# A diffusion backbone on one core: where the modulation steps stand in VectorE's order, where one of their vectors is computed, and which queue loads their tiles

## Chip, cores and metric

The kernel runs on one core of a Trainium2 chip. The metric is device microseconds of one execution; the median of three runs of the kernel before is 2502.87 us (2501.15 to 2503.94). A profile is one further execution, taken by the hardware profiler; it has its own time.

Five engines matter: TensorE (PE, matmuls; PEld is its weight load), VectorE (DVE), ScalarE (ACT), GpSimd (POOL), which here does little but issue DMAs, and SyncE (SP), which issues nearly all other DMAs. Each runs its own instructions in the order in which they were laid down and waits on semaphores for the others.

## The reference, cut to what matters

Two layers over 512 latent and 256 context tokens of width 1024. Every sub-layer is an RMSNorm with a scale and a shift, a body, and a gated residual; shift, scale and gate come out of one product of a conditioning vector with a large matrix, `ada_w`:

```python
m_lat = (silu_c @ ada_w[i] + ada_b[i]).reshape(b, N_SUBLAYERS, N_MOD, 1, d)
m_ctx = (silu_cc @ ada_w[i] + ada_b[i]).reshape(N_SUBLAYERS, N_MOD, 1, d)
h = norm_modulate(x_lat, norm_g[i, 0], m_lat[:, 0, 0], m_lat[:, 0, 1])
x_lat = x_lat + MACARON_WEIGHT * m_lat[:, 0, 2] * swiglu(h, ffn_w_in[i, 0], ffn_w_out[i, 0])
```

Layer 0 is SwiGLU, short convolution, SwiGLU; layer 1 is SwiGLU, attention, SwiGLU. So there are 2 x 9 modulation vectors of 1024 numbers (shift, scale and gate of three sub-layers in two layers), each for two conditioning rows, latent and context, but for the last four of layer 1, which only the latent tokens need.

## The kernel before, in words

**Stages.** The program runs through six stages in this order: f00 (first SwiGLU), c01 (convolution), f02, f10 (SwiGLUs), attention, and the last SwiGLU. In the profile f00 ends near 585 us, c01 near 837, f02 near 1353, f10 near 1877 us; attention and the last SwiGLU follow.

**Products.** The four stages f00, c01, f02 and f10 go through `products` (from line 1014). A stage has column chunks of 128 outputs (22 in an FFN stage, 12 in the convolution). The first two or three chunks are done directly; each of the others is seven products, M1 to M7, in the manner of Strassen: 12 matmuls each over four 128-row blocks and three parts (high x high, high x low, low x high), 384 tokens wide. In a chunk's order M7, M4 and M3 come one chunk later than M1, M2, M5 and M6. In an FFN stage every product but M1, M5 and M6 is followed by an eviction on DVE: L1069 after M2, L1078 after M7, L1129 after M4, L1083 after M3. L1078 must be done before M4 goes on in the same PSUM bank; L1083 frees a bank of tag C.

**Second projections.** After two or four chunks (convolution: four of its own outputs) stands a step `out`: the second projection of what is ready, 8 output blocks in groups of 3, 3 and 2, each for the latent tokens (512 wide) and then the context tokens (256 wide). That makes six groups of matmuls with DVE evictions at L874. `out_steps` is a generator that yields after each of the six; `out_phase` runs it through.

**Weights.** SP loads raw weight tiles (L209, five buffers, 512 KB each). `split` (L179 on ACT, L180 on DVE) makes high and low parts, a granule; eight granules are held ahead of PE. L347 and L356 form the sums and differences that M3, M5 and M6 need. PE and SP keep the order of the program; DVE and ACT are ordered by a scheduler at build time, which lets an instruction go ahead as soon as it takes its inputs to be there.

**Modulation steps.** The 15 vectors that are not needed at the start are computed on DVE beside the products. A vector is 8 blocks of 128 outputs, each block in two halves of 512 inputs; a half block is one tile `aw` (128 x 512, 256 KB) and one or two steps, `ada_block` (line 497): L505 multiplies the tile with a conditioning row (`crow`) and adds up along the row, one step per conditioning row. A vector with two rows is 32 steps, with one row 16. `ADA_BY` (line 39) says how many of the 15 vectors are done by the end of a stage: 6 in f00, 4 more in f02, 5 more in f10; none in c01. `ADA_DEPTH` (line 40) is the number of tile buffers, 3 each. When the last step on a tile is traced, `ada_next` (line 490) issues the load that takes its buffer, on POOL's queue. Between the two halves stand 13 tasks that are no steps: the load of the other half of the rows, its Silu on ACT, and 11 that do nothing.

**Pace.** `bg` (line 554) is called once after every product and not in a second projection. From product 12 of the stage (its tiles are asked for two products sooner) to product `7 * (total - 2 - direct) - 1` it spreads the stage's tasks evenly: 205 tasks over 107 products in f00, 141 over 114 in f02, 109 over 114 in f10. Only the first step of a stage is pinned with `keep_in_program_order`, which puts an instruction behind the instruction that was traced on its engine just before; the others may be moved ahead or behind by the scheduler.

Of the kernel before, what the change touches and what calls it, by code (L numbers as in the profile page):

```python
# [9 lines left out]
F32 = mybir.dt.float32  # L10
# [7 lines left out]
P = 128  # L18
# [17 lines left out]

FFN_DIRECT, CONV_DIRECT, BOOT_DIRECT = 2, 3, 3

ADA_BY = {"f00": 6, "f02": 10, "f10": 15}
ADA_DEPTH = {"f00": 3, "f02": 3, "f10": 3}  # L40
HALF = D // 2
CONV_PARTS = (4, 4)
LAT, CTX = 0, 1
BOTH = ((0, NL), (NL, NX))
# [76 lines left out]
def backbone(ctx: ExitStack, tc: tile.TileContext, a: dict, out: bass.AP):  # L121
    nc = tc.nc
# [4 lines left out]
    tmp = ctx.enter_context(tc.tile_pool(name="tmp", bufs=4))  # L127
# [17 lines left out]
    def ptile(name, shape=(P, 512)):  # L145
        pool, tag = bank[name]
        return pool.tile(list(shape), F32, name=f"ps_{name}", tag=tag)
# [4 lines left out]
    vec, at = {}, 0  # L152
# [226 lines left out]
    def starts(parts):  # L379
        out = [0]  # L380
        for n in parts:
            out.append(out[-1] + n)
        return out
# [50 lines left out]
    ada_tasks, ada_range = {}, {}  # L434
# [53 lines left out]
    ada_blocks, ada_loaded, ahead = [], {}, {}  # L488

    def ada_next(n):  # L490

        if n < ahead["limit"]:
            i, m, k, c0 = ada_blocks[n]
            w = ada_loaded[n] = ahead["pool"].tile([P, HALF], F32, name=f"aw{i}_{m}_{k}_{c0}", tag="aw", bufs=ADA_DEPTH[ahead["key"]])
            nc.gpsimd.dma_start(w, a["ada_t"][i, m, k, :, c0 : c0 + HALF])  # L495

    def ada_block(n, v, nv):

        i, m, k, c0 = ada_blocks[n]
        w = ada_loaded[n]
        junk = w if v == nv - 1 else apool.tile([P, HALF], BF16, name=f"jk{n}", tag="acc")
        out = mods[i][:, m, k, v : v + 1]
        ins = dve.tensor_tensor_reduce(out=junk, in0=w, in1=ahead["rows"][:, v], scale=1.0, scalar=out if c0 else ada_b[:, i, m, k : k + 1], op0=ALU.mult, op1=ALU.add, accum_out=out)  # L505
        if pinned[0]:
            tc.keep_in_program_order(ins)
        pinned[0] = False
        if v == nv - 1:
            ada_loaded.pop(n)  # L510
            ada_next(n + ADA_DEPTH[ahead["key"]])
            if k == KC - 1 and c0:
                ada_done.update({(i, 2 * m), (i, 2 * m + 1)})

    def rows_load(c0):
        rows = ahead["rows"] = ahead["pool"].tile([P, 2, HALF], F32, name=f"crow{c0}", tag="crow")
        nc.gpsimd.dma_start(rows, a["c_rows"][:, c0 : c0 + HALF].partition_broadcast(P))

    def rows_silu():
        act.activation(ahead["rows"], ahead["rows"], AF.Silu)  # L520
# [1 line left out]
    def rest():  # L522
        pass

    pinned = [False]
    pace = {}

    def ada_list():

        vectors = [(i, m) for i in range(2) for m in range(9) if i or m > 2]  # L530
        t0 = 0
        for key, t1 in ADA_BY.items():
            first = len(ada_blocks)
# [9 lines left out]
            ada_range[key] = first, len(ada_blocks)  # L543
            t0 = t1

    def bg_start(key, pool, first, last):

        pace.update(n=0, done=0, first=first, last=last, tasks=ada_tasks.pop(key, []))
        pace["steps"] = len(pace["tasks"])
        if pace["steps"]:  # L550
            ahead.update(pool=pool, key=key, start=ada_range[key][0], limit=ada_range[key][1])
        pinned[0] = True

    def bg():

        pace["n"] += 1
        if not pace["steps"]:
            return
        if pace["n"] == pace["first"] - 6:
            rows_load(0)  # L560
        if pace["n"] == pace["first"] - 2:
            rows_silu()
            for n in range(ADA_DEPTH[ahead["key"]]):
                ada_next(ahead["start"] + n)
        if pace["n"] < pace["first"]:
            return
        span = pace["last"] - pace["first"] + 1
        due = min(pace["steps"], -(-pace["steps"] * (pace["n"] - pace["first"] + 1) // span))
        while pace["done"] < due:
            pace["tasks"][pace["done"]]()  # L570
            pace["done"] += 1
# [10 lines left out]
    stage = {}  # L582
# [413 lines left out]
    def out_phase(*args):  # L996
        for _ in out_steps(*args):
            pass
# [15 lines left out]
    def products(gp, key, order, parts, direct, chunk, straight, out_args, after, passes, hooks, hold):  # L1014


        live = {}
        at = starts(parts)
        total = at[-1]
        pairs = [0]  # L1020
        bg_start(key, stage["aw"], 10 if key == "c01" else 12, 7 * (total - 2 - direct) - 1)

        def directly(n, c, m):
            half, kh = int(m[0]), int(m[1])
            st = live.setdefault(c, {"taken": {}, "used": {}})
            if kh not in st["taken"]:
                mark = len(taken)
                st[kh] = [w_get(0) for _ in range(2)]
                st["taken"][kh] = taken[mark:]
                del taken[mark:]  # L1030
            if kh == 0:
                st["ps", half] = [ptile(t, (P, NH)) for t in ("BS" if pairs[0] == 3 else "AC")]
                pairs[0] += 1
            xh, xl = T[f"B{kh + 1}{half + 1}"]
            for k in range(4):
                for (wh, wl), ps in zip(st[kh], st["ps", half]):
                    mm3(ps, wh[:, k, :], wl[:, k, :], xh[:, k, :], xl[:, k, :], kh == 0 and k == 0, kh == 1 and k == 3)
                if (n, k) in hooks:
                    hooks[n, k]()
                if k == 2 and half:  # L1040
                    w_fill(1)
            st["used"][kh] = st["used"].get(kh, 0) + 1
            if st["used"][kh] == 2:
                taken.extend(st["taken"][kh])
                w_done()
            if kh == 1:
                evictions.append(lambda ps=st["ps", half]: straight(c, half, ps))
                if n not in hold:
                    evict()

        def product(c, m):
            st = live.setdefault(c, {})
            _, tname, tag = PRODUCTS[m]
            first = m in ("M1", "M2", "M5")
            if first:
                st[tag] = ptile(tag, (P, NH))
            ps = st[tag]
            wh, wl = w_get()
            th, tl = T[tname]
            for k in range(4):  # L1060
                mm3(ps, wh[:, k, :], wl[:, k, :], th[:, k, :], tl[:, k, :], first and k == 0, k == 3, skip_group_check=True)
            w_done()
            if c == total - 1:
                traced.add((key, m))
            if m == "M1":
                st["g1"] = qp.tile([P, NH], F32, name="g1", tag="g1", bufs=2)
                act.activation(st["g1"], ps, AF.Copy)
            elif m == "M2":
                dve.tensor_tensor(out=st["g1"], in0=ps, in1=st["g1"], op=ALU.add)  # L1069
            elif m == "M5":  # L1070
                st["c22"] = qp.tile([P, NH], F32, name="c22", tag="c22", bufs=2)
                act.activation(st["c22"], ps, AF.Copy)
            elif m == "M6":
                st["g2"] = qp.tile([P, NH], F32, name="g2", tag="g2", bufs=2)
                act.activation(st["g2"], ps, AF.Copy)
                chunk(c, "c11", st)
            elif m == "M7":
                dve.tensor_tensor(out=st["c22"], in0=ps, in1=st["c22"], op=ALU.add)  # L1078
                chunk(c, "c22", st)
            elif m == "M4":  # L1080
                chunk(c, "c21", st)
            else:
                dve.tensor_tensor(out=st["g2"], in0=ps, in1=st["g2"], op=ALU.add)  # L1083
                chunk(c, "c12", st)
                live.pop(c)

        steps = [n for n, (c, m) in enumerate(order) if m != "out" and c < direct]
        for n, (c, m) in enumerate(order):
            if m == "out":
                last = c == len(parts) - 1  # L1090
                if last and isinstance(after, dict):
                    out_close(*out_args(c), after)
                else:
                    out_phase(BOTH, passes, *out_args(c), after if last else None, out_banks, 3)
                    if n in hooks:
                        hooks[n]()
                    for go in behind_outs:
                        go()
                    behind_outs.clear()
            elif c < direct:  # L1100
                directly(n, c, m)
            else:
                product(c, m)
                bg()
            if n in hooks and m != "out":
                hooks[n]()
            if n == steps[-1]:
                free_order()
# [692 lines left out]
```

## Time and profile before

| what | value |
|---|---|
| median of three runs | 2502.87 us (2501.15 to 2503.94) |
| the profiled execution | 2499.04 us, span 2497.3 us, mean granted clock 0.994 |
| PE busy | 2436.3 us of the span, 13632 matmuls |
| L505, modulation steps | 416 steps, median 745 ns; 240 tiles, 256 KB each |
| steps run | 152 to 472 us (f00), 914 to 1139 (f02), 1430 to 1619 (f10) |
| DVE waits for a tile's DMA | 16.8 us in 19 waits |
| SP's raw loads in f00, 150 to 480 us | waited 308.4 us for splits |
| POOL's instructions | 254, nearly all of them DMA issues |

How to read it: busy times of engines overlap, so no sum of them is the span. `out<-in` names what an instruction writes and reads. A row of waits has the waiting engine and line, the one that released it, the total, the number and the longest wait. A row of windows has the stretch, its length, the busy time (and count) of PE, PEld, DVE, ACT and POOL, the clock that PE was granted (1.00 is full), the DMA engines' busy share and GB/s. A time line row has the start, the length, the engine, the line and the operation, and in brackets the idle time before it and what ended it. `DVEq`, `SPq` and the like are an engine's sequencer, which issues DMAs and waits.

### The profile page before, as it was taken

What the parts mean: (1) busy time and instruction counts of PE and PEld (TensorE: products, weight loads), DVE (VectorE), ACT (ScalarE), POOL (GpSimd) and SP (SyncE); (2) the same over time, 40 slices, a digit from 0 to 9 for tenths busy, and PEclk for the clock granted to TensorE, in tenths of its full rate; (3) what the DMA queues carried; (4) which work ended last, traced back from release to release, by engine and by line L of the source; (5) the groups of instructions that cost most, each with busy time, mean ns of one, the idle gap of its engine ahead of it and who ended that gap; (6) DMA issues with size and microseconds to landing.
All of it is one profiled execution on the core that took longest, in us unless ns stands there. A gap on an engine that the chain in (4) does not pass through costs nothing.

```text
span 2497.3 us, 35662 instructions
## 1 busy us (share of the span) xinstructions
PE 2436.3 (98%) x13632; PEld 2263.3 (91%) x13632; DVE 1897.2 (76%) x3758; ACT 1094.2 (44%) x2016; POOL 135.1 (5%) x254
## 2 busy tenths in 40 slices
PE   6999999999999999999999999999999999999998
PEld 3889999999999999999999999899997889888887
DVE  4699999878968899996667989866668887544443
ACT  4443343355525643433435534244346775433233
POOL 0011111000000001110000021200000000000000
PEclk9999999999999999999999999999999999999999
DMA  7333543330213034533221155522231101332221
GB/s 276 110 125 116 165 155 129 110 110 26 76 51 117 28 106 148 161 123 102 85 74 49 67 172 167 183 79 68 68 110 60 43 18 60 102 101 93 96 82 34
DMA packets 92155, 252.53 MB, mean 101 GB/s; under 512 B 10192, under 2 KB 19536, under 8 KB 91984
## 3 DMA queue, kind: packets, MB, share of 16 engines
q1 hardware_dynamic: 71072, 183.00, 22.3%
q0 software_dynamic: 20064, 66.08, 8.2%
q8 instruction: 107, 1.75, 0.3%
q10 hardware_dynamic: 848, 1.18, 0.1%
q14 instruction: 64, 0.52, 0.1%
HBM read 248.11 MB, written 2.10 MB: 100 GB/s over the span
## 4 chain that ended last, share of the span: by engine, by line
PE 74%; issue 11%; DVE 8%; ACT 2%; POOL 2%; DMA 2%; SPq 0%; POOLq 0%; DVEq 0%; ACTq 0%
PE ps_A L809 14%; PE ps_A L808 14%; PE ps_A L810 14%; PE ps_C L808 7%; PE ps_C L810 7%; PE ps_C L809 7%; POOL aw L495 2%; PE ps_B L810 2%; PE ps_B L809 2%; PE ps_B L808 2%; DVE w L180 2%; DVE aw L505 1%; DVE jk L505 1%; PE ps_T L1481 1%; DVE x L874 0%
## 5 line engine op out<-in xcount | busy, mean ns | idle before, releaser
L179 ACT ACTIVATE w<-raw 128x512 fp32r<-128x512 f32 (+2 forms) x810 | 491.5, 618 | 752.4 <-PE ps_A L810 460.3
L180 DVE TENSOR_TENSOR w<-raw,w 128x512 fp32r<-128x512 f32 (+2 forms) x810 | 541.2, 677 | 183.9 <-ACT w L179 175.2
L809 PE MATMUL ps_A<-gl,w 128*128 128x512 f32 (+2 forms) x624 | 212.6, 341 | 0.4 <-DVE gl L180 0.4
L808 PE MATMUL ps_A<-gh,w 128*128 128x512 f32 (+2 forms) x624 | 212.1, 340 | 0.1
L810 PE MATMUL ps_A<-gh,w 128*128 128x512 f32 (+2 forms) x624 | 212.0, 340 | 0.0
L495 POOL DMA_DIRECT2D aw<-in_ada_t x240 | 129.6, 540 | 1130.5 <-DVE mods L505 1109.6
L874 DVE SCALAR_TENSOR_TENSOR x<-ps_A,gat,x 128x512 f32<-128x512 f32 (+1 forms) x192 | 118.6, 619 | 79.7 <-PE ps_A L810 79.5
L808 PE MATMUL ps_C<-gh,w 128*128 128x512 f32 (+1 forms) x472 | 166.6, 353 | 9.1 <-DVE g L1083 8.8
L809 PE MATMUL ps_C<-gl,w 128*128 128x512 f32 (+1 forms) x472 | 165.9, 352 | 0.0
L810 PE MATMUL ps_C<-gh,w 128*128 128x512 f32 (+1 forms) x472 | 165.7, 351 | 0.0
L809 PE MATMUL ps_A<-hl,w 128*128 128x512 f32 (+1 forms) x424 | 162.6, 384 | 2.4 <-DVE hl L668 2.4
L808 PE MATMUL ps_A<-h,w 128*128 128x512 f32 (+1 forms) x424 | 162.2, 382 | 1.0 <-DVE x L874 1.0
L810 PE MATMUL ps_A<-h,w 128*128 128x512 f32 (+1 forms) x424 | 162.1, 382 | 0.0
L347 DVE TENSOR_TENSOR raw<-raw,raw 128x512 f32<-128x512 f32 x204 | 139.5, 687 | 8.8 <-DMA raw<-in_ffn_w_in 6.3
L809 PEld LDWEIGHTS ps_A<-gl,w 128*128 128x128 f32 x624 | 118.6, 190 | 16.0 <-DVE gl L180 1.9
L808 PEld LDWEIGHTS ps_A<-gh,w 128*128 128x128 f32 x624 | 118.5, 190 | 15.2 <-ACT gh L179 1.0
L810 PEld LDWEIGHTS ps_A<-gh,w 128*128 128x128 f32 x624 | 118.6, 190 | 12.9
L874 DVE SCALAR_TENSOR_TENSOR x<-ps_C,gat,x 128x512 f32<-128x512 f32 (+1 forms) x136 | 87.7, 645 | 52.0 <-PE ps_C L810 51.8
L808 PEld LDWEIGHTS ps_C<-gh,w 128*128 128x128 f32 x472 | 90.0, 191 | 22.5 <-issue 11.3
L808 PE MATMUL ps_A<-tB11h,w 128*128 128x384 f32 x312 | 106.9, 343 | 3.0 <-ACT tB11h L763 2.9
L809 PE MATMUL ps_A<-tB11l,w 128*128 128x384 f32 x312 | 106.1, 340 | 0.3 <-DVE tB11l L765 0.3
L810 PE MATMUL ps_A<-tB11h,w 128*128 128x384 f32 x312 | 105.7, 339 | 0.0
(426 smaller groups left out, 6623.9 us busy)
## 6 DMA issues: line engine op xcount, KB each, us to landing
raw<-in_ffn_w_in SPq DMA_DIRECT2D x174, 512.0 KB, 3.7
aw<-in_ada_t POOLq DMA_DIRECT2D x240, 256.0 KB, 3.2
raw<-in_ffn_w_out SPq DMA_DIRECT2D x76, 512.0 KB, 3.9
raw<-in_conv_w_in SPq DMA_DIRECT2D x24, 512.0 KB, 3.7
ada<-in_ada_w SPq DMA_DIRECT2D x27, 256.0 KB, 6.0
raw<-in_attn_w_qkv SPq DMA_DIRECT2D x12, 512.0 KB, 4.8
raw<-in_ada_w SPq DMA_DIRECT2D x8, 512.0 KB, 5.2
raw<-in_conv_w_out SPq DMA_DIRECT2D x8, 512.0 KB, 3.7
```

The costliest lines, as they stand in the source:

```text
L179: act.activation(dsth, src, AF.Copy)
L180: dve.tensor_tensor(out=dstl, in0=src, in1=dsth.bitcast(F32), op=ALU.subtract)
L347: dve.tensor_tensor(out=quad(o), in0=quad(x), in1=quad(y), op=ALU.subtract)
L495: nc.gpsimd.dma_start(w, a["ada_t"][i, m, k, :, c0 : c0 + HALF])
L505: ins = dve.tensor_tensor_reduce(out=junk, in0=w, in1=ahead["rows"][:, v], scale=1.0, scalar=out if c0 else ada_b[:, i, m, k : k + 1], op0 ...
L808: pe.matmul(ps, wh, xh, start=first, stop=False, **kw)
L809: pe.matmul(ps, wh, xl, start=False, stop=False, **kw)
L810: pe.matmul(ps, wl, xh, start=False, stop=last, **kw)
L874: dve.scalar_tensor_tensor(out=x, in0=p[:, o - off : o - off + w], scalar=gat[:, m, v : v + 1], in1=x, op0=ALU.mult, op1=ALU.add)
L1481: pe.transpose(pt[:, c, :], pr[:, (c0 + c) * P : (c0 + c + 1) * P], ident)
```

## The change

1. The vectors are divided otherwise: 5 in f00, 1 in c01, 4 in f02, 5 in f10. c01's tiles use two buffers of an existing pool (tag `r`).
2. Every step is pinned behind what was traced before it on DVE, not only the first of a stage.
3. `bg` is also called after each of the six groups of a second projection. A stage's tasks are spread over weights: 1 for each product, 6 and 3 in turn for the latent and the context group.
4. A tile's load is issued on SP's queue, not POOL's, and at the next call of `bg` (or when it is needed), not with the step that frees its buffer. The row loads (`crow`) stay on POOL's queue.

```diff
-ADA_BY = {"f00": 6, "f02": 10, "f10": 15}
-ADA_DEPTH = {"f00": 3, "f02": 3, "f10": 3}
+ADA_BY = {"f00": 5, "c01": 6, "f02": 10, "f10": 15}
+ADA_DEPTH = {"f00": 3, "c01": 2, "f02": 3, "f10": 3}
+OUT_WEIGHT = (6, 3)
...
-            w = ada_loaded[n] = ahead["pool"].tile([P, HALF], F32, name=f"aw{i}_{m}_{k}_{c0}", tag="aw", bufs=ADA_DEPTH[ahead["key"]])
-            nc.gpsimd.dma_start(w, a["ada_t"][i, m, k, :, c0 : c0 + HALF])
+            pool, tag = (tmp, "r") if ahead["key"] == "c01" else (ahead["pool"], "aw")
+            w = ada_loaded[n] = pool.tile([P, HALF], F32, name=f"aw{i}_{m}_{k}_{c0}", tag=tag, bufs=ADA_DEPTH[ahead["key"]])
+            nc.sync.dma_start(w, a["ada_t"][i, m, k, :, c0 : c0 + HALF])
...
+        while n not in ada_loaded:
+            ada_next(ada_freed.pop(0))
...
-        if pinned[0]:
-            tc.keep_in_program_order(ins)
-        pinned[0] = False
+        tc.keep_in_program_order(ins)
         if v == nv - 1:
             ada_loaded.pop(n)
-            ada_next(n + ADA_DEPTH[ahead["key"]])
+            ada_freed.append(n + ADA_DEPTH[ahead["key"]])
...
-    def bg():
-
-        pace["n"] += 1
+
+    def bg(at):
+
+        while ada_freed:
+            ada_next(ada_freed.pop(0))
         if not pace["steps"]:
             return
-        if pace["n"] == pace["first"] - 6:
+        first = min(pace["slots"])
+        if at == (first[0] - 6, 0):
             rows_load(0)
-        if pace["n"] == pace["first"] - 2:
+        if at == (first[0] - 2, 0):
             rows_silu()
             for n in range(ADA_DEPTH[ahead["key"]]):
                 ada_next(ahead["start"] + n)
-        if pace["n"] < pace["first"]:
-            return
-        span = pace["last"] - pace["first"] + 1
-        due = min(pace["steps"], -(-pace["steps"] * (pace["n"] - pace["first"] + 1) // span))
+        pace["now"] += pace["slots"].get(at, 0)
+        due = min(pace["steps"], -(-pace["steps"] * pace["now"] // pace["total"]))
         while pace["done"] < due:
             pace["tasks"][pace["done"]]()
             pace["done"] += 1
...
-        bg_start(key, stage["aw"], 10 if key == "c01" else 12, 7 * (total - 2 - direct) - 1)
+        begin, end = 10 if key == "c01" else 12, 7 * (total - 2 - direct) - 1
+        slots, count = {}, 0
+        for c, m in order:
+            if m == "out":
+                if begin <= count <= end:
+                    slots.update({(count, 1 + q): OUT_WEIGHT[q % 2] for q in range(6)})
+            elif c >= direct:
+                count += 1
+                if begin <= count <= end:
+                    slots[count, 0] = 1
+        bg_start(key, stage["aw"], slots)
+        traced_products = 0
...
-                    out_phase(BOTH, passes, *out_args(c), after if last else None, out_banks, 3)
+                    steps_of = out_steps(BOTH, passes, *out_args(c), after if last else None, out_banks, 3)
+                    for q, _ in enumerate(steps_of):
+                        bg((traced_products, 1 + q))
...
                 product(c, m)
-                bg()
+                traced_products += 1
+                bg((traced_products, 0))
```

More of the change, by code (lines that the diff above doesn't have):

```diff
@@ L523, in rest @@
         pass
-    pinned = [False]
+    ada_freed = []
     pace = {}
@@ L544, in ada_list, with bg_start @@
             t0 = t1
[L546 to L550, printed above, removed]
+    def bg_start(key, pool, slots):
+        tasks = ada_tasks.pop(key, [])
+        pace.update(tasks=tasks, steps=len(tasks), done=0, now=0, slots=slots, total=sum(slots.values()))
+        if tasks:
             ahead.update(pool=pool, key=key, start=ada_range[key][0], limit=ada_range[key][1])
-        pinned[0] = True
-    def bg():
-        pace["n"] += 1
+    def bg(at):
+        while ada_freed:
+            ada_next(ada_freed.pop(0))
         if not pace["steps"]:
             return
-        if pace["n"] == pace["first"] - 6:
+        first = min(pace["slots"])
+        if at == (first[0] - 6, 0):
             rows_load(0)
-        if pace["n"] == pace["first"] - 2:
+        if at == (first[0] - 2, 0):
             rows_silu()
```

## The prediction

> **What bounds the kernel now.** I read the page first (parts 1 and 2), then who TensorE (PE) waited for, stage by stage, then the time line of VectorE (DVE) just before PE's longest waits.
>
> ```profile
> PE 2436.3 (98%) x13632; PEld 2263.3 (91%) x13632; DVE 1897.2 (76%) x3758; ACT 1094.2 (44%) x2016; POOL 135.1 (5%) x254
> DVE  4699999878968899996667989866668887544443
> ```
>
> PE is busy for 98% of 2497.3 us, so an edit on DVE can win only PE's waits and the slow matmuls after them. The digits show DVE full in slices 3 to 7 (125 to 437 us, stage f00) and around slices 14 to 17 and 22 to 24 (f02, f10): the three stages that carry modulation steps. PE's waits on DVE in these stages (f00 150 to 480, f02 840 to 1120, f10 1400 to 1620 us; columns: total, times, longest):
>
> ```profile
> PE ps_A L808 <- DVE c L1078: 3.6, 1, 3.6
> PE ps_C L808 <- DVE g L1083: 2.6, 2, 2.2
> ...
> PE ps_C L808 <- DVE g L1083: 1.3, 1, 1.3
> ...
> PE ps_C L808 <- DVE g L1083: 4.9, 2, 3.8
> PE ps_A L808 <- DVE c L1078: 1.1, 1, 1.1
> ```
>
> That is 6.2 + 1.3 + 6.0 = 13.5 us. Both lines are evictions of a product, L1078 for M7 and L1083 for M3. PE waits again for the first when it begins M4, two products later; for the second when the second projection, which follows M3 at once, wants its second C bank. Why L1083 is late, from DVE's time line before the 3.8 us wait:
>
> ```profile
> 1561.02 0.74 DVE L505 CUSTOM_DVE_ANT_0 aw<-aw,crow,mods 128x512 f32<-128x512 f32 x1
> 1561.69 0.08 DVE L505 DVE_READ_ACCUMULATOR2_ANT mods<- 128x1 f32 x1
> 1561.69 0.55 DVE L1078 TENSOR_TENSOR c<-ps_A,c 128x384 f32<-128x384 f32 x1
> ...
> 1568.00 0.75 DVE L505 CUSTOM_DVE_ANT_0 aw<-aw,crow,mods 128x512 f32<-128x512 f32 x1 [1.48 <-DMA aw<-in_ada_t]
> 1568.68 0.08 DVE L505 DVE_READ_ACCUMULATOR2_ANT mods<- 128x1 f32 x1
> 1568.68 0.68 DVE L180 TENSOR_TENSOR w<-raw,w 128x512 fp32r<-128x512 f32 x1
> 1569.28 0.75 DVE L505 CUSTOM_DVE_ANT_0 aw<-aw,crow,mods 128x512 f32<-128x512 f32 x1
> ...
> 1572.17 0.55 DVE L1083 TENSOR_TENSOR g<-ps_C,g 128x384 f32<-128x384 f32 x1
> ```
>
> A step (L505) takes 0.67 us from its start to the next (1561.02 to 1561.69). Steps stand ahead of evictions that PE needs, and one of them sat 1.48 us waiting for its own tile with the queue behind it.
>
> A wait also slows the matmuls after it. Windows over the ends of three waits (columns: length, PE, PEld, DVE, ACT, POOL busy, granted clock, DMA share, GB/s):
>
> ```profile
> 178.40:181.40 3.00, 2.95 (x9) 2.95 (x10) 3.00 (x8) 0.00 (x0) 1.01 (x2) 0.50 0.51 167
> 188.00:191.50 3.50, 3.50 (x10) 2.68 (x11) 3.50 (x9) 0.81 (x2) 0.54 (x1) 0.55 0.24 77
> 1573.00:1578.00 5.00, 5.00 (x16) 3.92 (x17) 3.44 (x9) 0.80 (x2) 1.61 (x3) 0.66 0.87 298
> ```
>
> Lost work: 3.0 x 0.50 + 3.5 x 0.45 + 5.0 x 0.34 = 1.5 + 1.6 + 1.7 = 4.8 us. With the waits, 18.3 us are at stake. The middle window follows the 2.2 us wait. By the Trainium skill ("TensorE: Matmul & The Clock Gate", Part 1: The HAM clock gate) the clock halves only after an idle window of about 3.4 us; by that rule this 1.6 us would not belong to the wait and the stake would be 16.7 us. This trace does not agree, since its clock is 0.55 right behind a wait of 2.2 us, so I keep 18.3.
>
> **Pace and load, before and after.** Between its two halves a stage has 13 tasks that are no steps. Before, the tasks of a stage fell evenly on its products: f00 had 6 vectors x 32 steps + 13 = 205 tasks on 107 products, 1.92 each; f02 141 on 114, 1.24; f10 109 on 114, 0.96. After, each product is a slot of weight 1 and the six groups of a second projection weigh 6 and 3 in turn, 27 a projection: f00 has 173 tasks on 107 + 4 x 27 = 215, 0.80 a unit; f02 141 on 222, 0.64; f10 109 on 222, 0.49; c01, new, 45 on 39 + 27 = 66, 0.68. What room there is shows where no steps run: products just before f00's steps, f00's end, a second projection of f10, products of c01 (three rows).
>
> ```profile
> 110.00:150.00 40.00, 40.00 (x230) 38.06 (x229) 38.25 (x63) 20.61 (x38) 0.00 (x0) 1.00 0.13 48
> ...
> 500.00:540.00 40.00, 40.00 (x230) 40.00 (x229) 26.98 (x45) 19.22 (x37) 0.00 (x0) 1.00 0.31 93
> 1666.00:1699.00 33.00, 33.00 (x193) 29.23 (x192) 17.91 (x30) 5.94 (x10) 0.00 (x0) 1.00 0.10 33
> ...
> 650.00:670.00 20.00, 20.00 (x116) 20.00 (x115) 18.59 (x41) 8.86 (x17) 0.00 (x0) 1.00 0.21 73
> 670.00:690.00 20.00, 20.00 (x114) 19.79 (x113) 15.79 (x41) 10.88 (x22) 0.00 (x0) 1.00 0.45 131
> 750.00:770.00 20.00, 20.00 (x115) 20.00 (x115) 19.05 (x50) 11.11 (x24) 0.00 (x0) 1.00 0.34 105
> ```
>
> Products of an FFN stage: 230 matmuls in 40 us, 0.174 us each, 12 a product, so 2.09 us a product, of which DVE is busy 67%; 0.68 us are free. Before, the steps asked 1.92 x 0.67 = 1.29 us in f00 (overload), 0.83 in f02 (overload), 0.64 in f10 (just under, and there the tile came late). After: 0.54, 0.43 and 0.33 us. All fit. A second projection (192 matmuls) lasts 33 us, of which DVE has 33 - 17.9 = 15.1 free; in f00 it gets 27 x 0.80 = 21.7 steps, 14.5 us: it fits, but only just, with up to 5 steps in a row behind three evictions. In f02 and f10 it gets 11.6 and 8.9 us. So:
>
> - f00: DVE no longer falls behind. DVE is nearly full just before the steps begin (38.25 of 40 us), so I leave 1 us of its 6.2 + 3.1 us (bounds 0 and all of it).
> - f02 and f10: nothing is left of 1.3 and 6.0 + 1.7 us. With 0.49 tasks a unit a new tile is needed every 4.3 us in f10's products and three are in flight, so the 1.48 us kind of wait goes too.
> - c01: 16 of the 32 steps fall before the stage's only second projection in range and around its start, the 13 other tasks mostly into it, and 16 behind it. A step costs 0.68 x 0.67 = 0.46 us of each 2.09 us, 22%, and DVE is 93 to 95% busy without it in 650 to 670 and 750 to 770. From 657 to 690 the steps need 7.2 us and find about 0.9 + 4.2 = 5.1: a lag of 2 us at the projection. There L1083 has six matmuls of 0.23 us (the starts in the rows below), 1.4 us, before PE wants its bank, so some 1 us is lost. In 750 to 770 they need 4.4 and find 0.95: a lag of 3.4 us, under the 4.2 us (M5 and M6) that L1078 has. Price 1 us; bounds 0 and 2.0 + 3.4 = 5.4.
>
> ```profile
> 1568.45 0.39 PE L809 MATMUL ps_A<-gl,w 128*128 128x512 f32 x1
> 1568.68 0.39 PE L810 MATMUL ps_A<-gh,w 128*128 128x512 f32 x1
> ```
>
> **Tiles by the sync queue.** 240 loads leave POOL's queue for SP's. SP's queue runs in program order and waits nearly always:
>
> ```profile
> SPq L209 <- DVE w L180: 308.4, 44, 25.2
> ...
> raw<-in_ffn_w_in SPq DMA_DIRECT2D x174, 512.0 KB, 3.7
> aw<-in_ada_t POOLq DMA_DIRECT2D x240, 256.0 KB, 3.2
> ```
>
> The first row is f00, 150 to 480 us: SP waits 308.4 us of 330 for the split that frees a raw buffer. A tile load now waits on SP for the last step on its buffer, with the weight loads of the next products queued behind it, and those splits and so PE behind them. I price this at nothing: the load is traced one call after the step, and the raw load behind it needs a split that comes after that step in any case. The cover is the eight granules of lead, seven products or 14.6 us; if it goes, PE waits for weights. In the other direction, a tile is reloaded one product later than now (2.1 us) and lands 3.2 us on; with depth 3 in f00 the next use is two blocks, 10 us, away, and with depth 2 in c01 about 9 us. POOL is then left with six row loads, which wait for nobody.
>
> The start of the program also changes. POOL's first tile loads run ahead of everything today:
>
> ```profile
> 2.48 1.62 POOL L495 DMA_DIRECT2D aw<-in_ada_t  x3
> ...
> 8.00:12.00 4.00, 0.05 (x1) 0.08 (x2) 0.16 (x1) 2.41 (x4) 0.00 (x0) 1.00 1.01 359
> ...
> PE ps_C L471 <- DMA ada<-in_ada_w: 12.0, 1, 12.0
> ```
>
> Three loads of 256 KB (786 KB in all) go out at 2.48 us, while PE's first matmul waits 12.0 us for a DMA and the DMA engines are full (share 1.01, 359 GB/s). In SP's order they come with f00's tenth product. They take 786 / 359 = 2.2 us of full DMA out of the front. PE's first 20 us are paced by these landings, so I take 1.5 us; bounds 0 and 2.2.
>
> **The sum.** 18.3 - 1 (f00) - 1 (c01) + 1.5 (start) = 17.8 us. The profiled execution took 2499.04 us (span 2497.3 and 1.7 around it), so it becomes 2481.2. It lies 3.8 us below the median of the three timed runs, 2502.87; off that median the forecast is 2485. Bounds: best 18.3 + 2.2 = 20.5, 2482; with small unlisted waits also gone, 2478. Worst, with 5.4 in c01, 9.3 in f00 kept and nothing at the start, 3.6 us won: 2499.
>
> **Rivals.**
>
> *DVE keeps its lag.* The pins hold a step behind what was traced before it, and evictions behind the step. If DVE enters f00's first projection late as now and c01 pays its 5.4, the gain is 4 to 10 us: 2493 to 2499. For it: the full DVE of 110 to 150 us, and 14.5 of 15.1 us in f00's projections. Against it: the load per product in f00 falls from 1.29 to 0.54 us.
>
> *The change only moves the waits.* The pins make the five steps of a burst precede the next evictions, and each of the 13 second projections in range begins with 1.3 us of waiting, as f02's one does: 13 x 1.3 = 17 us lost, as much as won; 2500 to 2506. Against it: the 15.1 us that DVE has free in a second projection, and f10's and f02's small share of it.
>
> *Slower: a tile load stands on SP behind a blocked raw load.* In c01 SP sits through about 13 us between pairs of raw loads. If a tile's load is queued behind such a wait, its step is late by 13 less the 3.6 us that depth 2 leaves, 9.6 us, and evictions stand behind the pinned step with 4.2 us of cover: 9.6 - 4.2 = 5.4 us for each of some six column chunks in range, 32 us, against the 17.8: 2517. It decides from the point at which the wait passes 3.6 + 4.2 = 7.8 us. SP's rows speak for it:
>
> ```profile
> SPq L209 <- DVE w L180: 83.5, 11, 25.0
> SPq L209 <- DVE cy L1196: 20.3, 3, 13.2
> ```
>
> (c01, 650 to 775 us.) Against it: the blocked raw load is traced where its buffer is freed, behind the tile loads of the calls before.
>
> *The steps do not move* (other pins decide the order already): within 2 us of now. The diff pins every step, so this gets little.
>
> **Chances.** Forecast (gain over 12 us) 0.58; lag kept 0.18; waits moved or nothing moved 0.12; SP or another new wait 0.12. A difference under 0.2%, 5 us, is about what a measurement of this kernel cannot tell from none, so faster means below 2497.9. Nearly all of the first two cases lies there: faster 0.75, same 0.13, slower 0.12. Range 2478 to 2503: it holds the first two cases and the better half of the third, and leaves out some 0.15.
>
> **What the changed profile should show.** 160, 32, 128 and 96 steps of L505 in f00, c01, f02 and f10, reaching to some 520, 770, 1300 and 1830 us; no PE wait on L1078 or L1083 over 1 us in f00, f02, f10; no clock under 0.9 after 110 us in them; ada loads of the start landing some 2 us earlier; fewer 9s on DVE in f00's slices. The forecast is wrong if PE shows waits over 2 us in 650 to 780, if DVE waits for the tile's DMA more than its 16.8 us of now, or if ACT or DVE wait for raw loads in the middle of a stage.
>
> ```profile
> DVE aw L505 <- DMA aw<-in_ada_t: 16.8, 19, 2.4
> ```

## The result and the profile after

The changed kernel takes 2478.01 us, the median of four runs (2476.31 to 2480.77), against 2502.01 us for the kernel before. The ratio is 0.9906, 95% interval 0.9888 to 0.9923. Its profiled execution took 2477.58 us with a span of 2475.8, so the two profiles differ by 21.5 us; the other 2.5 us of the medians' 24.0 are not in them, as the profiled execution of the kernel before lies 3 us below its median. The page's first part shows little of that. PE's busy time fell by 5.4 us, and DVE did the same 3758 instructions:

```profile
PE 2430.9 (98%) x13632; PEld 2261.2 (91%) x13632; DVE 1891.7 (76%) x3758; ACT 1093.9 (44%) x2018; POOL 7.1 (0%) x16
```

The page's chain that ended last says more. Before, its engine shares were these:

```profile
PE 74%; issue 11%; DVE 8%; ACT 2%; POOL 2%; DMA 2%; SPq 0%; POOLq 0%; DVEq 0%; ACTq 0%
```

After, nearly all of the chain is PE:

```profile
PE 94%; DVE 2%; ACT 2%; DMA 1%; issue 0%; SPq 0%; DVEq 0%; ACTq 0%
```

PE's waits from 110 to 1900 us, all four rows that there are before:

```profile
PE ps_C L808 <- DVE g L1083: 8.8, 5, 3.8
PE ps_A L808 <- DVE c L1078: 4.7, 2, 3.6
PE ps_A L808 <- DVE x L874: 1.0, 1, 1.0
PE ps_C L808 <- DVE x L874: 0.2, 1, 0.2
```

And all that there are after (L875 is the eviction of a second projection, L874 before; L1090 and L1095 are now the evictions after M7 and M3, which were L1078 and L1083):

```profile
PE ps_A L809 <- DVE x L875: 1.0, 1, 1.0
PE ps_Q L1370 <- DVE tl L620: 1.0, 1, 1.0
```

The two evictions are gone as releasers. Where the time was won is read from PE's time line, by when the same matmul starts in both. Each row is the first matmul of a second projection: the first of f00, the last of f00, the first of f02, the last of f02, the last of f10. Before:

```profile
113.63 0.39 PE L808 MATMUL ps_C<-gh,w 128*128 128x512 f32 x1
...
550.70 0.34 PE L808 MATMUL ps_C<-gh,f00held 128*128 128x384 f32 x1
...
875.22 0.40 PE L808 MATMUL ps_C<-gh,w 128*128 128x512 f32 x1
...
1318.69 0.34 PE L808 MATMUL ps_C<-gh,f02held 128*128 128x384 f32 x1
...
1842.16 0.40 PE L808 MATMUL ps_C<-gh,f10held 128*128 128x512 f32 x1
```

After:

```profile
112.42 0.39 PE L809 MATMUL ps_C<-gh,w 128*128 128x512 f32 x1
...
539.46 0.34 PE L809 MATMUL ps_C<-gh,f00held 128*128 128x384 f32 x1
...
864.32 0.40 PE L809 MATMUL ps_C<-gh,w 128*128 128x512 f32 x1
...
1305.91 0.34 PE L809 MATMUL ps_C<-gh,f02held 128*128 128x384 f32 x1
...
1820.38 0.40 PE L809 MATMUL ps_C<-gh,f10held 128*128 128x512 f32 x1
```

The changed kernel is ahead by 1.2, 11.2, 10.9, 12.8 and 21.8 us at these points. So 1.2 us come from the start, 10.0 from f00, -0.3 from c01, 1.9 from f02 and 9.0 from f10, and the last 650 us give nothing. A stage's length below is the time from one of these five marks to the next. All kernels here run 13632 matmuls, and the same ones serve as marks in each, in one profiled execution per kernel.

The windows of f00, f02 and f10 after (columns as in the prediction):

```profile
150.00:480.00 330.00, 330.00 (x1884) 315.32 (x1883) 290.03 (x624) 122.48 (x227) 0.72 (x1) 1.00 0.40 128
840.00:1120.00 280.00, 280.00 (x1596) 269.85 (x1595) 240.06 (x466) 123.57 (x228) 0.72 (x1) 1.00 0.32 103
1400.00:1620.00 220.00, 220.00 (x1257) 212.38 (x1256) 175.51 (x339) 89.51 (x166) 0.73 (x1) 1.00 0.39 126
```

PE never idles in them and the granted clock is 1.00 throughout. For f00 the same window before reads:

```profile
150.00:480.00 330.00, 323.71 (x1826) 308.94 (x1825) 318.52 (x721) 124.87 (x227) 50.93 (x94) 0.99 0.45 146
```

DVE was busy for 318.5 of 330 us, 97%, and is now at 290.0, 88%, while PE gets through 58 more matmuls in the same 330 us. That is the stage reading in one line: not less work for DVE in all, but less of it in this window. The direction of waiting at an f10 projection has turned round as well. DVE's time line just before it, in the kernel after:

```profile
1551.61 0.56 DVE L1095 TENSOR_TENSOR g<-ps_C,g 128x384 f32<-128x384 f32 x1 [0.29 <-PE ps_C L811]
```

This is the place where PE had waited 3.8 us for the eviction of M3. Now the eviction waits 0.29 us for PE.

DVE's waits for loads, 110 to 1900 us, after:

```profile
DVE raw L348 <- DMA raw<-in_ffn_w_in: 20.0, 14, 2.9
DVE aw L509 <- DMA aw<-in_ada_t: 1.1, 2, 0.7
```

The steps' tiles come in time (16.8 us of waits before), but the raw weight loads now come later. They stand on SP behind loads of tiles, as SP's waits in 150 to 480 us show:

```profile
SPq L497 <- DVE mods L509: 189.4, 60, 7.9
SPq L210 <- DVE w L181: 91.9, 36, 12.6
```

Before, SP waited 308.4 us there for splits alone. The 20 us of waits for raw tiles reach nobody: PE has no wait behind them, since eight granules lie ahead of it.

### The profile page after: what moved, and what is told of

It reads as the page before. It is cut to its first block, busy times and chain, and to the rows that moved or that the text cites. A ratio compares the mean times of both kernels' runs of the same rounds, so it can differ in the third digit from the quotient of the medians.

```text
span 2475.8 us, 35587 instructions
## 1 busy us (share of the span) xinstructions
PE 2430.9 (98%) x13632; PEld 2261.2 (91%) x13632; DVE 1891.7 (76%) x3758; ACT 1093.9 (44%) x2018; POOL 7.1 (0%) x16
## 4 chain that ended last, share of the span: by engine, by line
PE 94%; DVE 2%; ACT 2%; DMA 1%; issue 0%; SPq 0%; DVEq 0%; ACTq 0%
PE ps_A L810 18%; PE ps_A L809 18%; PE ps_A L811 18%; PE ps_C L809 9%; PE ps_C L810 9%; PE ps_C L811 9%; PE ps_B L811 3%; PE ps_B L810 3%; PE ps_B L809 3%; PE ps_T L1496 1%; DMA ada<-in_ada_w 0%; ACT pr L1480 0%; PE ps_C L1473 0%; PE ps_O L809 0%; PE ps_O L811 0%
## 5 line engine op out<-in xcount | busy, mean ns | idle before, releaser
L875 DVE SCALAR_TENSOR_TENSOR x<-ps_A,gat,x 128x512 f32<-128x512 f32 (+1 forms) x192 | 118.8, 621 | 60.9 <-PE ps_A L811 60.3
L875 DVE SCALAR_TENSOR_TENSOR x<-ps_C,gat,x 128x512 f32<-128x512 f32 (+1 forms) x136 | 87.8, 646 | 68.6 <-PE ps_C L811 68.4
L811 PE MATMUL ps_C<-tB22h,w 128*128 128x384 f32 x296 | 100.0, 338 | 0.0
```

The costliest lines, as they stand in the source:

```text
L811: pe.matmul(ps, wl, xh, start=False, stop=last, **kw)
L875: dve.scalar_tensor_tensor(out=x, in0=p[:, o - off : o - off + w], scalar=gat[:, m, v : v + 1], in1=x, op0=ALU.mult, op1=ALU.add)
```

## The experiments

Theory 1 is the prediction's: what matters is DVE's room, per product and per second projection, and the change wins because it puts the steps where there is room. The rival, theory 2: the order alone does it, since a pinned step can't float ahead of an eviction that PE needs. Times are medians of four or more runs, beside the kernel before on the same chip (2501.4 to 2501.9 in the three sets).

**The order alone.** The kernel before with every step pinned, at its old pace:

```diff
-        if pinned[0]:
-            tc.keep_in_program_order(ins)
+        tc.keep_in_program_order(ins)
```

> The kernel before with every step pinned behind what was traced before it, and nothing else. Theory 1 (room: the waits come from steps asking more of VectorE per product than the 0.68 us that are free): pins make no room, 1.92 steps x 0.67 = 1.29 us a product stay in f00, now without the freedom to run ahead, so VectorE falls behind by 0.6 us a product and the projections give back some 15 us of it: slower than before, 2510 to 2550. Theory 2 (order: the waits come from steps that stood ahead of evictions, whatever the load): most of the gain, 2480 to 2488.

It took 2531.4 us (2529.0 to 2533.3), ratio 1.0116 [1.0100, 1.0133]: 30 us slower. PE's waits, 110 to 1900 us:

```profile
PE ps_C L807 <- DVE g L1082: 28.1, 10, 8.3
PE ps_A L807 <- DVE c L1077: 11.5, 6, 5.6
```

The waits on the same two evictions (one line up in this kernel) are three times those of before. At the old pace f00's steps ask 1.29 us of the 0.68 us that a product leaves, and pinned they can't slide into the projections: 32 of f00's 192 steps begin while PE is in a second projection, where in the kernel before 71 do. Stage by stage the order is not worthless. f00 is 36.2 us longer than before and f02, which asks 0.83 us, 1.3 us longer; but f10, whose old pace asks 0.64 us and fits, is 5.2 us shorter. Theory 2 falls as the whole cause: pins lose where the pace doesn't fit, and win where it does.

**The queue alone.** The kernel before with its tile loads on SP:

```diff
-            nc.gpsimd.dma_start(w, a["ada_t"][i, m, k, :, c0 : c0 + HALF])
+            nc.sync.dma_start(w, a["ada_t"][i, m, k, :, c0 : c0 + HALF])
```

> The kernel before with the tile loads on the sync queue, and nothing else. Theory 1 (room): the steps ask as much as before; only the start gains, 1.2 us, so 2497 to 2502. Theory 3 (queue: the late tiles of GpSimd's queue and VectorE's 16.8 us of waiting for them were the cause): most of the gain, 2480 to 2488, and VectorE's wait for tiles near 0.

It took 2513.4 us (2511.5 to 2520.6), ratio 1.0053 [1.0037, 1.0068], which neither theory had. The steps now run from 152 to 538, 930 to 1298 and 1448 to 1817 us, where before they ended at 472, 1139 and 1619. SP issues in program order, so a tile can't land ahead of its turn, and the unpinned steps are held to the program's pace through their data. That pace overloads DVE:

```profile
PE ps_A L808 <- DVE c L1078: 11.5, 5, 4.3
PE ps_C L808 <- DVE g L1083: 11.3, 6, 3.0
```

Here too f00 loses (16.7 us) and f10 wins (3.7 us). So "the queue" isn't a matter of the queue's speed; it is a weaker kind of pin. This run is also the first sign that the scheduler of the kernel before did not keep to the program's pace.

**The new pace without pins**, tiles on SP:

```diff
-        tc.keep_in_program_order(ins)
+        if not pinned:
+            tc.keep_in_program_order(ins)
+        pinned.append(n)
...
-    ada_freed = []
+    ada_freed, pinned = [], []
...
+        pinned.clear()
```

(The last line stands in `bg_start`, so the first step of a stage stays pinned, as before.)

> The changed kernel with only the first step of a stage pinned. Theory 1 (room): the load fits and the tiles come in the sync queue's program order, so the steps cannot run far ahead: 2476 to 2481, no waits on products' evictions. Theory 2 (order): steps run ahead of evictions again and 8 to 20 us come back, 2486 to 2498.

2483.5 us (2479.6 to 2485.1), ratio 0.9926 [0.9911, 0.9941]: between the two expectations. Without pins the steps run ahead until they stand at their tiles, on DVE (`jk` and `aw` are the steps' outputs):

```profile
DVE jk L509 <- DMA aw<-in_ada_t: 51.6, 37, 3.4
DVE aw L509 <- DMA aw<-in_ada_t: 18.8, 19, 3.5
```

70.4 us of DVE's time instead of 1.1, and evictions queue behind them: two waits of up to 2.1 us each on L1098 (M3's eviction) and L878 (a second projection's) came back on PE.

**The new pace alone**, the kernel of the last experiment with its tiles on POOL's queue:

```diff
-            nc.sync.dma_start(w, a["ada_t"][i, m, k, :, c0 : c0 + HALF])
+            nc.gpsimd.dma_start(w, a["ada_t"][i, m, k, :, c0 : c0 + HALF])
```

> The changed kernel with only the first step of a stage pinned and the tile loads on GpSimd's queue: the new pace and the vector in c01 alone. Theory 1 (room, with pins worth 5 us where tiles are late): tiles are not late on this queue, which waits for nothing but the steps, so steps that run ahead stand before evictions as they did, but half as many a product: 2480 to 2490. Theory 2 (order): most of the gain goes, 2492 to 2502.

2492.4 us (2490.7 to 2494.6), ratio 0.9963 [0.9950, 0.9975]. Theory 1 had 2480 to 2490 and missed. f02's steps ran from 906 to 1131 us and f10's from 1422 to 1615, as in the kernel before (914 to 1139, 1430 to 1619), though this program spreads them to about 1270 and 1790. PE's waits, 110 to 1900 us:

```profile
PE ps_C L812 <- DVE g L1098: 6.2, 3, 4.5
PE ps_A L812 <- DVE x L878: 2.6, 2, 1.6
PE ps_A L812 <- DVE c L1093: 1.9, 2, 1.5
```

A step that takes its inputs to be there goes ahead, whatever pace the program has. The pace alone saves 9.4 us. In the profile f00 has all that the change won there (9.9 us), f10 has none of it (3.6 us longer than before); what is missing needs something that holds the steps to the pace.

**Tiles back on POOL, with pins and pace**, the changed kernel with this same edit of the queue alone:

```diff
-            nc.sync.dma_start(w, a["ada_t"][i, m, k, :, c0 : c0 + HALF])
+            nc.gpsimd.dma_start(w, a["ada_t"][i, m, k, :, c0 : c0 + HALF])
```

> The changed kernel with the tile loads back on GpSimd's queue. Theory 1 (room): pace and pins are as in the changed kernel, so only the start is lost, 1.2 us: 2478 to 2481, no new waits on evictions. Theory 3 (queue): tiles come late again and stand in VectorE's queue, 5 us or more come back: 2483 to 2495.

2479.4 us (2478.1 to 2482.9), ratio 0.9914 [0.9897, 0.9932], with one wait of 1.1 us on the two evictions. The queue is worth 1.4 us here, and the two kernels' runs overlap, so it can't be told from none. The four kernels at the new pace, medians:

| | tiles on SP | tiles on POOL |
|---|---|---|
| every step pinned | 2478.0 (the change) | 2479.4 |
| only a stage's first step pinned | 2483.5 | 2492.4 |

Pins are worth 13 us with POOL and 5.5 with SP, which fits SP's order doing part of their work. At the old pace the same pins cost 30 us. No part has a price of its own. By stage, against the kernel before (us, one profile each):

| | f00 | c01 | f02 | f10 |
|---|---|---|---|---|
| the change | -10.0 | +0.3 | -1.9 | -9.0 |
| new pace alone | -9.9 | +2.0 | -0.4 | +3.6 |
| old pace, every step pinned | +36.2 | +0.5 | +1.3 | -5.2 |

So in f00 the new pace is enough, and in f10 it is the pins that win.

**Room in the products.** The change without the slots of the second projections:

```diff
-OUT_WEIGHT = (6, 3)
+OUT_WEIGHT = (0, 0)
```

> The changed kernel with weights 0 for the second projections, so that all steps stand at products. Theory 1 (room): f00 asks 173/107 x 0.67 = 1.08 us a product and c01 45/39 x 0.67 = 0.77 us where it has 0.1 to 0.4: 25 us lost in f00, 10 in c01, some 5 in f02 (0.83), none in f10 (0.64): 2505 to 2525. Theory 2 (order): pins are enough, 2478 to 2484.

2512.2 us (2511.6 to 2513.4), ratio 1.0043 [1.0028, 1.0058], as theory 1 had it. The first of PE's waits, 110 to 1900 us:

```profile
PE ps_C L809 <- DVE g L1095: 10.8, 7, 5.5
PE ps_A L809 <- DVE c L1090: 9.4, 9, 2.6
```

Pins and queue are those of the change; only the slots are missing, and 34 us with them. By stage f00 loses 24.8 us against the change, c01 4.5, f02 3.1 and f10 2.0.

**Room in the projections.** The other way round, four times the weight on them:

```diff
-OUT_WEIGHT = (6, 3)
+OUT_WEIGHT = (24, 12)
```

> The changed kernel with weights 24 and 12 in place of 6 and 3. Theory 1 (room, also in the projections: 15.1 us each): f00 puts 108 x 173/539 = 34.7 steps, 23.2 us, into a projection, f02 18.7 us, f10 14.4 us: 4 x 4 to 8 us lost in f00, 4 x 0 to 4 in f02, none in f10: 2494 to 2520. Rival: in a projection nothing waits soon for VectorE, so it may fall behind at no cost: 2476 to 2482.

2501.6 us (2497.7 to 2503.5), ratio 0.9997 [0.9988, 1.0007]. f00, where a projection was to hold 23.2 us of steps, loses 19.8 us against the change; f02, with 18.7 us, only 0.9, so the 15.1 us are not a sharp limit. The projections' room ends too, and now it is L1090, behind a projection full of steps, that is late (PE's first row):

```profile
PE ps_A L809 <- DVE c L1090: 10.9, 4, 3.8
```

**The convolution.** None of the vectors there, f00 with six:

```diff
-ADA_BY = {"f00": 5, "c01": 6, "f02": 10, "f10": 15}
+ADA_BY = {"f00": 6, "f02": 10, "f10": 15}
```

> The changed kernel with all six vectors in f00 and none in c01. Theory 1 (room): f00 asks 205/215 x 0.67 = 0.64 us a product of 0.68 and 25.7 steps x 0.67 = 17.2 us a projection of 15.1: 0 to 6 us lost in f00, nothing won in c01: 2478 to 2484. A rival, that the move to the convolution is what relieves f00: 9 us come back, 2487.

2478.65 us (2476.8 to 2479.3), ratio 0.9906 [0.9891, 0.9922]: the same as the change. With 205 tasks on 215 units, f00 asks 0.95 x 0.67 = 0.64 us a unit and still fits under 0.68. The 17.2 us a projection of the expectation were too many: 82 steps begin in f00's four projections, 13.7 us in each, under the 15.1. f00 is 1.6 us longer than in the change. Moving a vector to c01 bought nothing that the time of the whole shows. Two vectors there:

```diff
-ADA_BY = {"f00": 5, "c01": 6, "f02": 10, "f10": 15}
+ADA_BY = {"f00": 4, "c01": 6, "f02": 10, "f10": 15}
```

> The changed kernel with two vectors in c01 and four in f00. By the prediction's reading of c01's room: 77/66 = 1.17 tasks a unit, 0.78 us a product, so 12.4 us asked and 5.1 free in the 33 us before its projection and 7.5 asked and 0.95 free in 750 to 770: lags of 7.3 and 6.6 us against covers of 1.4 and 4.2, 5 to 12 us slower than the changed kernel, 2483 to 2490. Rival, that c01 has more room than the busy digits say, as its one vector cost nothing: 2477 to 2480.

2491.6 us (2491.1 to 2494.6), ratio 0.9965 [0.9952, 0.9978]: 13.6 us slower than the change and 1.6 above the range that was expected; c01 itself is 15.0 us longer. The first row of PE's waits:

```profile
PE ps_A L809 <- DVE c L1090: 9.0, 3, 6.2
```

So c01's room lies between one and two vectors.

**The rows' queue.** The change left the two kinds of loads on different queues. With the row loads on SP too:

```diff
-        nc.gpsimd.dma_start(rows, a["c_rows"][:, c0 : c0 + HALF].partition_broadcast(P))
+        nc.sync.dma_start(rows, a["c_rows"][:, c0 : c0 + HALF].partition_broadcast(P))
```

> The changed kernel with the conditioning rows (512 KB, out of the front of the program for f00) on the sync queue too. If the start is paced by the bytes in front of it: 512 KB at 359 GB/s are 1.5 us, of which the first 786 KB gave 1.2 of 2.2: 0.8 to 1.5 us faster than the changed kernel, 2476.5. Rival: the rows' load waits on the sync queue with weight loads behind it, in each of four stages: 0 to 10 us slower than the changed kernel.

2470.1 us (2468.6 to 2471.2), ratio 0.9873 [0.9857, 0.9889], 7.9 us better than the change and far more than expected. It has the lowest median of all kernels here. ACT's time line at the start shows why; after the change it is

```profile
13.40 1.28 ACT L522 ACT_TABLE_LOAD   x1
14.69 1.06 ACT L522 ACTIVATE crow<-crow 128x1024 f32<-128x1024 f32 x1
...
18.14 1.28 ACT L608 ACT_TABLE_LOAD   x1 [1.88 <-PE ps_S L627]
19.43 0.49 ACT L608 ACTIVATE y<-ps_S 128x384 f32<-128x384 f32 x1
19.94 1.28 ACT L609 ACT_TABLE_LOAD   x1
```

and with the rows on SP

```profile
17.71 0.49 ACT L608 ACTIVATE y<-ps_S 128x384 f32<-128x384 f32 x1 [2.64 <-PE ps_S L627]
18.23 0.52 ACT L609 ACTIVATE y<-y 128x384 f32<-128x384 f32 x1
```

Nothing stands ahead of the rows on POOL's queue (their load goes out at 1.29 us), and the scheduler lets their Silu (L522), traced ten products into f00, go ahead into the norms at the start. There it costs its own table load and makes the norm's L608 and L609 load theirs again, twice: 18 table loads in the program against 13. Five of 1.28 and the Silu's 1.06 are 7.5 us, and the first projection starts at 104.92 us instead of 112.42. By the Trainium skill ("ScalarE: Activation LUTs", What ACT_TABLE_LOAD costs) a load takes about 1283 ns and a drain of some 1380 ns comes with it, 2.66 us a switch. The trace has the 1.28 us but no room for the drain: L608's load ends at 19.42 and its activation begins at 19.43. Bytes taken out of the start were the other possible cause, so the Silu was pinned with the rows still on POOL:

```diff
-        act.activation(ahead["rows"], ahead["rows"], AF.Silu)
+        tc.keep_in_program_order(act.activation(ahead["rows"], ahead["rows"], AF.Silu))
```

> The changed kernel with the rows' Silu on ScalarE pinned behind what was traced before it; the rows' load stays on GpSimd's queue at the front. Theory A (tables: with the rows on the sync queue the start lost five ScalarE table loads of 1.28 us and a Silu of 1.06 us, which stood between the norm's square sums and its root): the same five loads go here, 6 to 7.5 us faster than the changed kernel, 2470.5 to 2472. Theory B (bytes: the 512 KB of rows in front of the program were what cost): no more than 1 us faster, 2477 to 2478.

2471.4 us (2470.6 to 2472.4), ratio 0.9881 [0.9867, 0.9896], with 13 table loads and the first projection at 105.40 us: it is the tables, for 6.6 of the 7.9 us. The other 1.3 us may be the bytes or scatter; the runs of the two kernels overlap. The kernel before has the same 18 loads and the same slip, so its rows were moved to SP as well (the same edit as for the rows above):

> The kernel before with the rows' load on the sync queue, and nothing else. Theory A (tables): the start's five table loads go here too, 6 to 8 us faster than before, 2493.5 to 2495.5, and the waits on L1078 and L1083 stay. Theory B (bytes): 1 us or less, 2500.5 to 2502.

2492.9 us (2490.8 to 2497.5), ratio 0.9966 [0.9956, 0.9976]: 9 us won between the medians, 6.1 of them by the first projection in the profile (107.53 us instead of 113.63), and PE's waits on the evictions stay, so the two gains are apart:

```profile
PE ps_C L808 <- DVE g L1083: 9.7, 5, 3.0
PE ps_A L808 <- DVE c L1078: 4.3, 1, 4.3
```

## Why the prediction was right, and what was off

The mechanism was right: the waits of PE on the two evictions went, in f00, f02 and f10, with the slow matmuls after them, and nothing took their place. The gain is 24.0 us between the medians (21.5 between the profiles) against 17.8 forecast. The sum's own best case was 2482; 2478.01 lies inside the range only by the allowance for small waits that were not listed, and by 0.01 us, which is luck. Term by term:

- *The stake, 18.3 us, was too small.* The stages f00, f02 and f10 gave 20.9. The waits were counted as PE's idle time, but what a wait costs is the delay of the next matmul. In the row below (before) the idle time is 3.79 us; the matmul ahead of it began at 1568.68, and a normal pitch is 0.23, so the start came 3.95 us late. Taken so from PE's time line, the gaps over 0.6 us lose 14.7 us where 13.5 were counted. The slow matmuls that remain, those over 0.3 us apart, lose about 6 where 4.8 were counted in three windows: 4.8 us are those at the half clock, read rightly, and 11 more at the full clock lose the rest.

```profile
1572.86 0.47 PE L808 MATMUL ps_C<-gh,w 128*128 128x512 f32 x1 [3.79 <-DVE g L1083]
```

- *f00's residue, 1 us, was 0.* DVE's being full before the steps did not matter.
- *c01's price, 1 us, was next to nothing.* c01 takes 324.9 us with its vector and 324.8 without one. The lag was read rightly as small. PE loses nothing in the windows with the highest load (after):

```profile
650.00:670.00 20.00, 20.00 (x116) 20.00 (x115) 19.64 (x44) 9.82 (x19) 0.00 (x0) 1.00 0.51 158
670.00:690.00 20.00, 20.00 (x115) 18.39 (x114) 17.23 (x51) 6.86 (x15) 0.00 (x0) 1.00 0.39 121
750.00:770.00 20.00, 20.00 (x115) 20.00 (x115) 19.56 (x52) 10.37 (x21) 0.00 (x0) 1.00 0.19 57
```

  DVE is busy for 98% of 650 to 670 and 750 to 770 us, and by the prediction's reading the cover of two products takes up the rest. With one vector more c01 is 15.0 us longer.
- *The start, 1.5 us, is 1.2 in the profiles.* The first matmul begins at 9.7 us instead of 12.0, but the first projection only 1.2 earlier. With tiles on SP and the rows on POOL as in the change, seven kernels have that projection at 112.21 to 114.51 us, mean 113.1 (two vectors in c01: 114.51); the four with tiles on POOL have it at 113.63 to 114.53, mean 114.1. So the term is about 1 us, and the scatter is as large. The start held a larger cost that the prediction did not see, the five table loads.
- *SP's queue at nothing was right*, but one sign that was named against the forecast did appear, waits for raw loads in mid-stage (3.1 us before, 20.0 after), and meant nothing: PE has no wait behind them. The rival of a tile load behind a blocked raw load fell with it.
- *The steps' ends* came at 512, 761, 1273 and 1789 us, earlier than the 520, 770, 1300 and 1830 that were named; the counts of 160, 32, 128 and 96 are as forecast. POOL is left with eight row loads, not six, since c01 has two of its own.

One step of the argument was right in its result and wrong in its reason. It took the steps of the kernel before to run at the program's pace, 1.92, 1.24 and 0.96 tasks a product. The scheduler moved them: f02's 128 steps ended at 1139 us where the program spreads them to about 1300, and pinned to that same pace the kernel is 30 us slower. Counted by what PE was doing when each step began (and a product as 2.09 us), the kernel before ran 1.21, 1.13 and 1.02 steps a product in f00, f02 and f10, the new pace alone 1.12, 1.11 and 1.01, and the change 0.81, 0.60 and 0.40; the 0.68 us of room are 1.01 steps of 0.67 us. So f00's overload before was 0.81 us of 0.68, not 1.29. Unpinned on POOL's queue, the steps run at the limit of the room or above it at either pace of the program, and the change holds them under it.

What the change does is therefore two things, neither of which gives the whole gain alone: a pace that fits, and pins that make it hold. The reading of room stands, by the runs that fill the products (+34 us over the change), the projections (+24) and c01 (+13.6).

Left open: why the new pace alone is enough in f00, where its steps still run at 1.12 a product while 1.21 cost 10.0 us; whether SP's queue is worth its 1.4 us, and what sets the microsecond or so by which the first projection's start varies.

## What to carry to other kernels

When background work shares an in-order engine with evictions, work out the room it has in each kind of slot, spread it by that room, and only then pin it: pins at an overloading pace cost 30 us here, and the fitting pace without pins got 9.4 of 24. A pace written in the program is only real if something holds it, a pin or an in-order queue that brings the data; check it by where the instructions ran in the trace. And look at what else a scheduler may move early: one Silu that slipped into the start cost five table loads on ACT, some 7 us, which a change of queue or one pin gave back.

## What the hardware showed

The clock's answer to a wait is not set by its length alone. In the attention the same matmul waits 2.39 us in both kernels. Before, it is followed by the full clock (the time line's row, then two windows, the wait's end lying in the second):

```profile
1970.63 0.50 PE L1458 MATMUL ps_C<-kh,qh 128*128 128x512 f32 x1 [2.39 <-ACT pr L1465]
...
1966.67:1970.09 3.42, 1.57 (x10) 1.22 (x8) 3.41 (x8) 1.22 (x3) 0.00 (x0) 1.00 0.48 150
1970.09:1973.50 3.41, 2.87 (x19) 2.60 (x20) 2.43 (x6) 3.04 (x7) 0.00 (x0) 1.00 0.48 154
```

After, by half of it:

```profile
1948.80 0.80 PE L1473 MATMUL ps_C<-kh,qh 128*128 128x512 f32 x1 [2.39 <-ACT pr L1480]
...
1945.25:1948.67 3.42, 1.16 (x7) 0.82 (x6) 3.00 (x7) 1.22 (x5) 0.00 (x0) 1.00 0.39 134
1948.67:1952.08 3.41, 3.28 (x13) 2.99 (x13) 1.90 (x4) 2.30 (x5) 0.00 (x0) 0.50 0.43 154
```

The windows are cut where the clock can change. In each of this case's 14 traces all changes of the granted clock lie on one grid of 3.41 us, and what differs is how the wait falls on it: before, 1.85 us of it in one window and the rest in the next; after, 2.26 us in one. Over all 14 traces, from 110 us to 10 us before the end, 29 windows at the full clock are followed by one at half, and PE was idle in them for 1.81 us or more. In the 9654 that are followed by the full clock it was idle for 1.85 us at most. So in these runs some 1.8 us of idle time within one window halve the next one, and that costs 3.41 x 0.50 = 1.7 us beside the wait; a wait of 2.39 us can cost it or not. In f00, f02 and f10 the kernel before has three such half windows, from 178.09, 188.33 and 1574.14 us, and the changed one none.

The Trainium skill ("TensorE: Matmul & The Clock Gate", Part 1: The HAM clock gate) says that the clock looks at free-running windows of 3413 ns; the grid in these traces agrees with that. Its idle window of about 3.4 us as the condition for the half clock does not hold as a lower bound: 1.8 to 2.3 us was enough here, and the prediction was right to keep the 1.6 us behind its wait of 2.2.

A tile's load (256 KB, median of 240) took 3.0 to 3.2 us from POOL's queue and 2.7 from SP's in the change; with tiles on SP and the steps not all pinned it took 3.7 and 3.9. All of it is too little to matter with two or three buffers.
